# SBUF buffers of a two-layer decoder trunk placed in a stated order, at chosen residues modulo 256 bytes

## The chip, the cores and the metric

The kernel runs on one core of one Trainium2 chip. The time is the device time of one execution in microseconds (us); the kernel before has 1070.82 us as the median of three runs (1070.0 to 1071.1).

## What is computed

The reference is a decoder trunk of two layers over 256 tokens of width 1024, in float32. Each layer merges three token mixers (a convolution module, a top-k sparse attention and a short gated convolution) and adds a gated feed-forward block:

```python
def hybrid_layer(x, ...):
    h = rms_norm(x, norm1_g)
    proj = h @ w_in                      # q, k, v, iq, ik, iw, a, c, g
    ...
    y_attn = dsa_attention(q, k, v, iq, ik, iw) @ w_attn_out
    y_conf = jax.nn.silu(layer_norm(a, conf_ln_g, conf_ln_b)) @ w_conf_out
    y_sc = (c_b * causal_dwconv(c_c * c_x, sc_conv_w)) @ w_sc_out
    merged = gates[:, :, 0] * y_conf + gates[:, :, 1] * y_attn + gates[:, :, 2] * y_sc
    x = x + merged @ w_o
    u = causal_dwconv(rms_norm(x, norm2_g) @ w_up, ffn_conv_w) + ffn_conv_b
    u_gate, u_val = jnp.split(u, 2, axis=-1)
    return x + (jax.nn.silu(u_gate) * u_val) @ w_down
```

All weights together are about 187 MB, and each is read once.

## The kernel before

**Tiles and stages.** Activations stand with features on the 128 partitions and the 256 tokens along the free axis. Every large product is a sum of 128x128 weight tiles times a 128x256 activation tile. The weights come from HBM as a stream of chunks of 128 x 2048 float32 (1 MB each), and each chunk is handled as two halves of eight tiles. ScalarE rounds a half to float32r (`cast`, L406, tile `wh`), VectorE takes the rest (`low`, L363, tile `wl` = raw - wh), and TensorE forms high x high, low x high and high x low, so that three matmuls stand for one float32 product (`fm`). In nearly all stages the weight tile is the stationary operand, which a LDWEIGHTS loads, and the activation tile is the moving one, 256 columns. In the stages IQ, KX, V and Q the two change places.

**Names.** The letters of the matmuls' outputs are the stages: A, IQ, KX, V, Q, C, CB, S, G, T, F, O, U, N, in this order in each layer. The moving tiles are `xgh/xgl` (input of a norm, high and low), `hh/hl` (normed), `sh/sl`, `ah/al`, `cfh/cfl`, `mh/ml` and `uh/ul`.

**Order of the work.** `Plan.add` records every instruction with its inputs, outputs, a cost and a due time, and `Plan.schedule` makes one list schedule of them for PE, ACT, DVE and the DMA queue of SP. A buffer (`Buf`) has a tag, and the schedule gives it a slot of this tag when its first instruction is issued: `raw` has 3 slots, `wh` 6, `wl` 6 (always used in the same turn, `wh_i` with `wl_i`), `big` 8 (activations of 8 KB per partition), `att` 2. `Plan.emit` then asks the tile pool for each buffer under the name of its slot, and writes out the instruction.

**Where a slot stands.** The pool lays its slots one behind another in SBUF, in the order in which a name is first asked for, each start at a multiple of 32 bytes. Before the change this is the order in which the schedule first uses a slot, so that small buffers stand between the large ones. Every address that a matmul reads is a slot's start plus a multiple of 256 bytes (a weight tile is 512 bytes per partition, an activation tile 1024), so that the start of the slot modulo 256 is the residue of all tiles in it. The stage KX is the exception: its tiles are 328 columns (1312 bytes) wide.

Of the kernel before, what the change touches and what calls it, by code (L numbers as in the profile page):

```python
# [9 lines left out]
F32 = mybir.dt.float32  # L10
# [6 lines left out]
P = 128  # L17
# [48 lines left out]
         "m8": 2, "tv": 3, "ty": 3, "tt": 3, "r2": 2, "two": 7, "one": 9, "mx": 2, "sm": 2, "ri": 2}  # L66
SHARED = {"m1": ("one", 5), "rr": ("one", 3), "b1": ("one", 2), "m2": ("two", 3), "rel": ("two", 2), "b2": ("two", 2), "ct": ("two", 2)}
BANKS = ("pm", "pq", "pa")
LOADS = {AF.Sigmoid: "sigmoid", AF.Exp: "exp", AF.Silu: "silu"}
LAT = {("dve", "dve"): 127, ("dve", "act"): 130, ("act", "act"): 143, ("act", "dve"): 143,  # L70
       ("dve", "pe"): 365, ("act", "pe"): 390, ("pe", "dve"): 198, ("pe", "act"): 198, ("pe", "pe"): 0,
# [7 lines left out]


class Buf:
    """A tile of the plan: placed in a slot of its tag when its first instruction is issued."""

    def __init__(self, shape, dtype, tag, name):
        self.shape, self.dtype, self.tag, self.name = list(shape), dtype, tag, name
        n = int(np.prod(shape[1:]))
        grain = n if tag in BANKS else (1 if n <= 64 else 64)
        self.idx = np.arange(n).reshape(shape[1:]) // grain
# [9 lines left out]


class View:  # L100
    """An access pattern of a Buf, built when the instruction is emitted."""

    def __init__(self, buf, chain, idx, shape=None, whole=False):
        self.buf, self.chain, self.idx, self.whole = buf, chain, idx, whole
# [35 lines left out]


class Plan:
    """Records instructions in program order, orders them by a list schedule, and emits them."""

    def __init__(self):
        self.ops = []
# [7 lines left out]
    def add(self, eng, fn, outs, ins, cost, func=None, due=None):  # L154
# [16 lines left out]
        for v in ins:  # L171
            if isinstance(v, View):
                b = v.buf
                op.bufs.append(b)
                bank = b.tag in BANKS
                for c in v.cells():
# [30 lines left out]
    def schedule(self):  # L207
# [51 lines left out]
        while len(done) < len(ops):  # L259
# [25 lines left out]
            cost = o.cost  # L285
            if o.func in LOADS and LOADS[o.func] != table:
                table = LOADS[o.func]
                cost += 1283
# [18 lines left out]
        return done  # L307

    def emit(self, tc, pools):
        for o in self.schedule():  # L310
            for b in o.allocs:
                b.tile = pools[b.tag in BANKS].tile(b.shape, b.dtype, tag=b.slot, name=b.name)
            o.fn()
# [3 lines left out]
def trunk(ctx: ExitStack, tc: tile.TileContext, xt: bass.AP, wst: bass.AP, prm: bass.AP,  # L317
# [39 lines left out]
    def psum(v):  # L357
        return isinstance(v, View) and v.buf.tag in BANKS

# [825 lines left out]
```

## Time and profile before

| | |
|---|---|
| median of 3 runs | 1070.82 us (1070.0 to 1071.1) |
| profiled execution, span from first to last instruction | 1068.2 us |
| PE busy | 1061.8 us, 99% of the span, 8784 matmuls |
| DVE busy | 914.3 us, 86% |
| ACT busy | 702.9 us, 66% |
| DMA | 191.63 MB, 179 GB/s on the mean |
| chain of waits that ended last | PE 98% |

The span is the time between the first and the last instruction of one profiled execution; the device time of a run also holds what lies around it. The page gives no device time of the profiled execution itself; the median of the runs is 2.6 us over its span. Matmuls are pipelined: the duration in a row of PE (some 280 ns) is a latency, and several overlap, so that the rate is read from the starts of successive rows of the timeline.

### The profile page before, as it was taken

To read this page: it belongs to the slowest core of one execution; us is meant where nothing else is said; L and a number is where in the kernel's file an instruction comes from. 1 tells how busy PE (TensorE), PEld (TensorE's weight loads), DVE (VectorE), ACT (ScalarE), POOL (GpSimd) and SP (SyncE) were. 2 spreads that over 40 slices of the span, in tenths; PEclk is the share of its full clock that TensorE was granted. 3 is DMA by queue.
4 is the path that set the end of the run, shared out by engine and by line. 5 is a ranking of instruction groups with operands and counts; after the bars stand their busy time and mean duration, and the time that the engine had idled before them with its cause. 6 is when DMAs were issued, how large, how long until landed. Compare 5 with 4: busy or idle time off the path is not lost.

```text
span 1068.2 us, 21702 instructions
## 1 busy us (share of the span) xinstructions
PE 1061.8 (99%) x8784; PEld 1046.6 (98%) x8784; DVE 914.3 (86%) x1813; ACT 702.9 (66%) x1242; POOL 0.2 (0%) x4
## 2 busy tenths in 40 slices
PE   8999999999999999999999999999999999999998
PEld 8999999999999999999999999999999999999998
DVE  7999999999887899885689999999987789988742
ACT  6868657896565666664466795588857456766531
POOL 0000000000000000000000000000000000000000
PEclk9999999999999999999999999999999999999999
DMA  8665554435655356555455554533464653655550
GB/s 286 222 208 176 170 165 156 153 119 182 214 198 198 119 198 219 182 199 201 171 175 184 205 182 146 201 133 119 163 233 156 204 193 120 222 212 184 179 211 21
DMA packets 29461, 191.63 MB, mean 179 GB/s; under 512 B 3504, under 2 KB 4784, under 8 KB 7088
## 3 DMA queue, kind: packets, MB, share of 16 engines
q1 hardware_dynamic: 29360, 190.23, 51.4%
q8 instruction: 69, 1.13, 0.4%
q14 instruction: 32, 0.26, 0.1%
HBM read 189.17 MB, written 1.05 MB: 178 GB/s over the span
## 4 chain that ended last, share of the span: by engine, by line
PE 98%; DVE 1%; DMA 1%; SPq 0%; issue 0%; ACT 0%; DVEq 0%
PE U L346 23%; PE G L346 13%; PE N L346 12%; PE C L346 9%; PE A L346 8%; PE T L346 4%; PE F L346 4%; PE O L346 4%; PE S L346 4%; PE Q L346 4%; PE CB L346 4%; PE IQ L346 2%; PE KX L346 1%; PE V L346 1%; PE qk L346 1%; PE po L346 1%
## 5 line engine op out<-in xcount | busy, mean ns | idle before, releaser
L363 DVE TENSOR_TENSOR wl<-raw,wh 128x1024 fp32r<-128x1024 f32 (+2 forms) x364 | 432.6, 1198 | 70.1 <-ACT wh L406 68.4
L406 ACT CAST wh<-raw 128x1024 fp32r<-128x1024 f32 (+2 forms) x364 | 369.1, 1030 | 165.6 <-PE N L346 39.5
L346 PE MATMUL U<-hhb,wh 128*128 128x256 f32 x576 | 139.1, 281 | 0.0
L346 PE MATMUL U<-hhb,wl 128*128 128x256 f32 x576 | 139.0, 280 | 0.0
L370 DVE SCALAR_TENSOR_TENSOR acc<-a,psb,acc 128x245 f32<-128x245 f32 (+18 forms) x320 | 132.3, 463 | 0.1
L346 PEld LDWEIGHTS U<-hhb,wl 128*128 128x128 f32 x576 | 108.7, 189 | 0.0
L346 PEld LDWEIGHTS U<-hhb,wh 128*128 128x128 f32 x576 | 108.5, 188 | 0.0
L346 PE MATMUL G<-hha,wh 128*128 128x256 f32 x384 | 94.0, 284 | 0.0
L346 PE MATMUL G<-hha,wl 128*128 128x256 f32 x384 | 92.8, 281 | 0.0
L346 PE MATMUL N<-uh,wh 128*128 128x256 f32 x352 | 83.0, 279 | 0.0
L346 PE MATMUL N<-uh,wl 128*128 128x256 f32 x352 | 83.0, 279 | 0.0
L346 PE MATMUL U<-hlb,wh 128*128 128x256 f32 x576 | 79.1, 280 | 0.0
L370 DVE SCALAR_TENSOR_TENSOR u<-U,psb,u 128x255 f32<-128x255 f32 (+1 forms) x144 | 59.6, 474 | 18.1 <-ACT u L401 18.1
L346 PEld LDWEIGHTS G<-hha,wl 128*128 128x128 f32 x384 | 72.7, 189 | 0.3 <-issue 0.2
L346 PEld LDWEIGHTS G<-hha,wh 128*128 128x128 f32 x384 | 72.5, 189 | 0.3 <-issue 0.2
L346 PEld LDWEIGHTS U<-hlb,wh 128*128 128x128 f32 x576 | 72.7, 188 | 0.0
L401 ACT ACTIVATE ct<-a,psb 128x253 f32<-128x253 f32 (+9 forms) x160 | 70.1, 489 | 0.0
L346 PEld LDWEIGHTS N<-uh,wl 128*128 128x128 f32 x352 | 66.5, 189 | 0.0
L346 PEld LDWEIGHTS N<-uh,wh 128*128 128x128 f32 x352 | 66.5, 189 | 0.0
L346 PE MATMUL C<-hha,wh 128*128 128x256 f32 x256 | 62.8, 285 | 0.0
L346 PE MATMUL C<-hha,wl 128*128 128x256 f32 x256 | 61.8, 280 | 0.0
L401 ACT ACTIVATE u<-U,psb 128x256 f32<-128x256 f32 x72 | 37.2, 560 | 34.3 <-PE U L346 34.3
(259 smaller groups left out, 2600.3 us busy)
## 6 DMA issues: line engine op xcount, KB each, us to landing
raw<-in_w SPq DMA_DIRECT2D x174, 1024.0 KB, 4.8
raw<-in_w SPq DMA_DIRECT2D x4, 656.0 KB, 3.9
raw<-in_w SPq DMA_DIRECT2D x8, 256.0 KB, 6.0
out<-xres SPq DMA_DIRECT2D x8, 128.0 KB, 2.1
xres<-in_xt SPq DMA_DIRECT2D x3, 256.0 KB, 6.3
psb<-in_p SPq DMA_DIRECT2D x2, 277.0 KB, 7.0
csb<-in_c SPq DMA_DIRECT2D x1, 304.0 KB, 8.5
xres<-in_xt SPq DMA_DIRECT2D x2, 128.0 KB, 3.6
```

Of the source, the lines that this page charges most:

```text
L346: nc.tensor.matmul(ap_of(o), ap_of(l), ap_of(r), start=st, stop=sp, skip_group_check=bool(kw))
L363: G.add("dve", lambda: nc.vector.tensor_tensor(ap_of(o), ap_of(a), ap_of(b), op=op), [o], [a, b], (c + n) / 0.96)
L370: G.add("dve", lambda: nc.vector.scalar_tensor_tensor(ap_of(o), ap_of(a), ap_of(s), ap_of(b), op0=op0, op1=op1), [o], [a, s, b], (c + n) / ...
L401: nc.scalar.activation(ap_of(o), ap_of(i), f, **{k: ap_of(v) for k, v in kw.items()})
L406: G.add("act", lambda: nc.scalar.copy(ap_of(o), ap_of(i)), [o], [i], width(o) / 1.2 + 94)
```

## The change

No computation is added, removed or reordered. `emit` first runs the schedule to its end, notes the largest size of each slot, and then asks the pool once for every slot in the order of the new table `LAYOUT`, with fillers between (`gap32` is 32 float32, 128 bytes); slots that the table doesn't name follow in the order of first use. After that the loop over the instructions runs as before and finds every slot at its place. The built programs of before and after have the same instructions in the same order on all five engines, row for row, with the same number of waits; the addresses alone differ.

```diff
@@ -66,6 +66,10 @@
 BANKS = ("pm", "pq", "pa")
+LAYOUT = (["gap32"] + [f"big_{i}" for i in range(4)],
+          ["gap32_b"] + [f"big_{i}" for i in range(4, 8)] + [f"att_{i}" for i in range(2)] + ["kT_0", "vt_0"],
+          ["gap32_c", "wh_0", "wl_0", "gap8_1", "wh_1", "wl_1", "gap8_2", "wh_2", "wl_2", "gap8_3", "wh_3", "wl_3"],
+          ["gap8_4", "wh_4", "wl_4", "gap16_5", "wh_5", "wl_5"])
@@ -307,7 +311,20 @@
     def emit(self, tc, pools):
-        for o in self.schedule():
+        order = self.schedule()
+        size = {}
+        for o in order:
+            for b in o.allocs:
+                if b.tag not in BANKS:
+                    n = int(np.prod(b.shape[1:]))
+                    size[b.slot] = max(size.get(b.slot, 0), n)
+        first = [t for group in LAYOUT for t in group]
+        for slot in first + [t for t in size if t not in first]:
+            if slot.startswith("gap"):
+                pools[0].tile([P, int(slot[3:].split("_")[0])], F32, tag=slot, name=slot)
+            elif slot in size:
+                pools[0].tile([P, size[slot]], F32, tag=slot, name=f"home_{slot}")
+        for o in order:
             for b in o.allocs:
                 b.tile = pools[b.tag in BANKS].tile(b.shape, b.dtype, tag=b.slot, name=b.name)
             o.fn()
```

The residues of the slots' starts modulo 256 bytes, from the two built programs (the eight big slots are named by the first tile that each holds in layer 0):

| slot | before | after |
|---|---|---|
| wh_0, wl_0 | 224, 224 | 0, 0 |
| wh_1, wl_1 | 224, 224 | 32, 32 |
| wh_2, wl_2 | 224, 224 | 64, 64 |
| wh_3, wl_3 | 224, 224 | 96, 96 |
| wh_4, wl_4 | 32, 160 | 128, 128 |
| wh_5, wl_5 | 224, 160 | 192, 192 |
| raw_0, raw_1, raw_2 | 192, 224, 224 | 0, 32, 32 |
| big_0, big_1 (xgh, xgl) | 224 | 0 |
| big_2, big_3 (hh, hl) | 160 | 0 |
| big_4, big_5, big_6 (a, acc, iq) | 160 | 128 |
| big_7 (qt) | 32 | 128 |
| att_0, att_1 (ah, al) | 32 | 128 |

TensorE reads two tiles at a time: the moving tile of the running matmul and the weights of the next one. Call **offset** the residue of the stationary tile that loads next minus the residue of the moving tile, modulo 256. Over the 8,205 neighbouring pairs of float32r matmuls with 256 columns the programs have

| offset | 0 | 32 | 64 | 96 | 128 | 160 | 192 | 224 |
|---|---|---|---|---|---|---|---|---|
| pairs before | 2600 | 0 | 3246 | 0 | 674 | 0 | 1685 | 0 |
| pairs after | 1361 | 787 | 1342 | 827 | 1356 | 595 | 1378 | 559 |

## Rows read from the trace of the kernel before

**Rows 1.** The page: span, busy time, granted clock in 40 slices, chain.
```profile
span 1068.2 us, 21702 instructions
...
PE 1061.8 (99%) x8784; PEld 1046.6 (98%) x8784; DVE 914.3 (86%) x1813; ACT 702.9 (66%) x1242; POOL 0.2 (0%) x4
...
PEclk9999999999999999999999999999999999999999
...
PE 98%; DVE 1%; DMA 1%; SPq 0%; issue 0%; ACT 0%; DVEq 0%
```
**Rows 2.** Waits of PE: who for whom, us in total, times, longest.
```profile
PE pw L346 <- DVE avg L506: 1.0, 1, 1.0
PE A L346 <- ACT xgha L401: 1.0, 1, 1.0
PE A L346 <- DVE wl L363: 0.9, 1, 0.9
```
**Rows 3.** Chain of waits: longest pieces; start us, us, what.
```profile
22.82 34.20 PE A L346 x288
236.44 36.84 PE G L346 x312
359.77 116.59 PE U L346 x992
476.36 61.58 PE N L346 x528
546.31 37.64 PE A L346 x320
886.89 116.71 PE U L346 x992
1003.60 61.43 PE N L346 x528
```
**Rows 4.** PE timeline, stage A, offset 0: start us, us, instruction.
```profile
27.27 0.28 PE L346 MATMUL A<-xgha,wl 128*128 128x256 f32 x1
...
39.86 0.28 PE L346 MATMUL A<-hha,wh 128*128 128x256 f32 x1
```
**Rows 5.** PE timeline, stage G, offset 64.
```profile
246.56 0.28 PE L346 MATMUL G<-hha,wl 128*128 128x256 f32 x1
...
258.93 0.28 PE L346 MATMUL G<-hha,wh 128*128 128x256 f32 x1
```
**Rows 6.** PE timeline, stage N, offset 64.
```profile
509.30 0.28 PE L346 MATMUL N<-uh,wh 128*128 128x256 f32 x1
...
512.02 1.18 PE L346 MATMUL N<-ul,wh 128*128 128x256 f32 x9
```
**Rows 7.** PE timeline, stage G, offset 128.
```profile
260.85 1.11 PE L346 MATMUL G<-hla,wh 128*128 128x256 f32 x8
261.80 0.28 PE L346 MATMUL G<-hha,wh 128*128 128x256 f32 x1
```
**Rows 8.** PE timeline, stage T of layer 1, offset 192.
```profile
810.55 0.28 PE L346 MATMUL T<-ah,wh 128*128 128x256 f32 x1
...
821.86 0.28 PE L346 MATMUL T<-ah,wh 128*128 128x256 f32 x1
```
**Rows 9.** PE timeline, stage KX (328 columns), every sixth matmul.
```profile
71.50 0.32 PE L346 MATMUL KX<-wh,hha 128*128 128x328 f32 x1
...
72.39 0.31 PE L346 MATMUL KX<-wh,hha 128*128 128x328 f32 x1
...
73.29 0.31 PE L346 MATMUL KX<-wh,hha 128*128 128x328 f32 x1
...
74.18 0.32 PE L346 MATMUL KX<-wh,hha 128*128 128x328 f32 x1
...
75.10 0.28 PE L346 MATMUL V<-wh,hha 128*128 128x256 f32 x1
```
**Rows 10.** PE timeline: first and last row of the float32r matmuls.
```profile
6.71 0.58 PE L346 MATMUL A<-xgha,wh 128*128 128x256 f32 x1 [1.04 <-ACT xgha L401]
...
1063.79 1.23 PE L346 MATMUL N<-ul,wh 128*128 128x256 f32 x9
```
**Rows 11.** Instructions that write wl and wh: duration ns min/median/max.
```profile
L363 DVE TENSOR_TENSOR wl<-raw,wh x364: 680/1217/1228, 6.0 to 1050.7; 128x1024 fp32r<-128x1024 f32 x174, 128x512 fp32r<-128x512 f32 x4, 128x656 fp32r<-128x656 f32 x4
L406 ACT CAST wh<-raw x364: 603/1047/1077, 5.3 to 1049.3; 128x1024 fp32r<-128x1024 f32 x174, 128x512 fp32r<-128x512 f32 x4, 128x656 fp32r<-128x656 f32 x4
```

## The prediction

> **What bounds the kernel now.** Read the page first [rows 1]: PE is busy 99% of the span, the chain that ended last is PE for 98%, and the granted clock is 9 in all forty slices, its upper level of 2.4 GHz. The waits of PE confirm it [rows 2]: three, 2.9 us together, all at the start. So no load, cast or subtraction holds TensorE up; the kernel is as long as 8,784 matmuls take one after the other. The chain shows at what pace [rows 3]: its seven longest pieces hold 3,960 matmuls in 464.99 us, 117.4 ns each, but they differ: 118.8 ns in the first piece of A, 118.1 in G, 117.5 in U, 116.6 and 116.3 in N. All are the same instruction, 128x128 weights and 256 columns. What differs is where their operands stand.
>
> The timeline of PE shows it, stretch by stretch. Take starts that follow each other and divide by the matmuls between them (counted in the program). Offset 0, stage A: 105 matmuls from 27.27 to 39.86, 119.9 ns each [rows 4]. Offset 192, stage T: 96 in 11.31 us, 117.8 ns [rows 8]. Offset 128: eight in 0.95 us, 118.8 ns [rows 7]. Offset 64 has two paces: 105 in 12.37 us, 117.8 ns, in G [rows 5], and 24 in 2.72 us, 113.3 ns, in N [rows 6]. Both kinds last for dozens of matmuls; which one a stretch falls into, the offset alone does not say.
>
> Over all starts between the first and the last row [rows 10], sorted by offset and without gaps over 140 ns (8,136 intervals), the means are 118.67 ns at offset 0 (2,562 of them), 116.23 at 64 (3,230), 118.93 at 128 (674) and 117.42 at 192 (1,670). I use these four; the stretches above show their spread.
>
> **The change part by part.** *Fillers and home tiles.* They issue no instruction: zero on every engine and queue.
>
> *Residues of raw, wh and wl for ScalarE and VectorE.* Before, `raw` stands at 192 and 224 and `wh` at 224 and 32, so VectorE already reads four combinations; yet its subtractions run 1217 ns in the median and 1228 at most, the casts 1047 and 1077 [rows 11]. They don't see residues. I cost this at nothing. The cover is PE: VectorE is busy 86% of the time, so that even 3% on each subtraction would still leave PE the bound.
>
> *Residues for TensorE.* This is the whole change, and its price is pairs times nanoseconds. Before: 2600 x 118.67 + 3246 x 116.23 + 674 x 118.93 + 1685 x 117.42 = 963.84 us. After, the four known offsets: 1361 x 118.67 + 1342 x 116.23 + 1356 x 118.93 + 1378 x 117.42 = 640.57 us for 5,437 pairs. Within them the trade is poor: 1,239 pairs leave the dear offset 0, but 1,904 leave 64, the cheapest, and 682 are added at 128, the dearest. The other 2,768 pairs go to 32, 96, 160 and 224, which no stage of this width has now. Their pace u decides: the break-even is (963.84 - 640.57) / 2768 = 116.8 ns.
>
> Bounds for u, from the nearest rows: below, 113.3 ns, the best pace held anywhere for a stretch [rows 6]; above, 119.9 ns, the worst [rows 4]. The first gives 640.57 + 313.61 - 963.84 = -9.7 us, the second 640.57 + 331.88 - 963.84 = +8.6 us. Between them I take the mean of the four known offsets, 117.8 ns, since each new one lies midway between two of them. That is +326.1 us, and the sum +2.8 us.
>
> One stage lets the new offsets be seen, at another width: in KX every second tile of 328 columns starts 32 bytes further round. In groups of six matmuls [rows 9] the first group (offsets 128 and 0) has 148 ns each, the second (96 and 224) 150, the third (192 and 0) 148, the fourth (160 and 224) 153. The new offsets are no cheaper there, rather 2 to 5 ns dearer. At 328 columns the load of the weights is hidden for longer, so I take the direction as a hint and not the size. It speaks against u near 113.
>
> Weigh this against a rule. The rows say that two tiles read at once cost each other up to 6.6 ns per matmul, by where they stand [rows 4, 6]. The Trainium skill says otherwise: "Loading the next tile's weights doesn't steal SBUF read bandwidth from the running matmul" (page "TensorE: Matmul & The Clock Gate", section "Step-by-step: what each phase is for"), because PE has two independent read ports. By that sentence the sum would be zero; by the rows it is +2.8 us. I go by the rows, since the same stationary and moving shapes at the same granted clock differ by 6%, and leave the rule as a rival.
>
> The sum is made on the profiled execution: 1068.2 + 2.8 = 1071.0 us of span. The median of the runs is 2.6 us over that span, so the forecast is 1073.6 us. A measurement of this kernel can tell about 0.2% (2.1 us) from no change, so the forecast stands just outside it.
>
> **The rivals.**
>
> *A, the new offsets are the good ones (faster).* The place is the 2,768 pairs at odd multiples of 32; the price is 2,768 x (116.8 - u), so that it decides from u = 116.0 downward, where the gain passes 2.1 us. At the fast pace of 113.3 the time is 1070.8 - 9.7 = 1061.1 us; if offset 64 also ran always at its fast pace, 1342 x (116.23 - 113.3) = 3.9 us more go, 1057.2. For it: the pace of 113.3 exists and holds for whole stretches, offset 64 and 192 both are cheaper than 0 and 128, so distance seems to help, and nothing shows that 64 is the best. Against it: KX, and that the new offsets are no farther apart than 64.
>
> *B, the new offsets are as dear as 0, and offset 64 loses its fast pace (slower by more).* 8.6 us from u = 119.9, and 1342 x (117.8 - 116.23) = 2.1 us from offset 64, together +10.7: 1081.5 us. For it: the fast stretch of N comes right behind one at offset 0 and lasts while the offset stays [rows 6]; six residues in turn change the offset every 24 matmuls. Against: it needs all new offsets to be at the worst value seen.
>
> *C, the pace does not hang on residues.* The differences would then be the stages' own, by order and neighbours, and the time stays at 1070.8 us. For it: offset 64 has two paces [rows 5, 6] with nothing moved. Against: offsets 0, 128 and 192 keep theirs in different stages of both layers. The skill's rule on the read ports, above, is this case.
>
> That the change doesn't do what it says I leave out: the built program has the stated residues.
>
> **How the numbers follow.** The forecast's own case is u between 116.0 and 118.8, -2.1 to +5.6 us, 1068.7 to 1076.4: 0.48, of which 0.20 within 0.2% and 0.28 slower. A has 0.34 (faster), B 0.12 (slower), C 0.06 (same). Hence faster 0.34, same 0.26, slower 0.40. The range reaches from A at its fast pace nearly to B: 1060 to 1080 leaves out the case that offset 64 gets fast as well, and the upper end of B.
>
> **What would show it.** Right: PE still 99% busy with no new wait; the paces of offsets 0, 128 and 192 within 1 ns of those above; stretches at 32, 96, 160 and 224 between 116 and 119 ns; subtractions still 1217 ns. The stages that had offset 64 most, G, C and O of layer 0, with weights now at six residues, lose a little of what the first A gains. Wrong: a stretch of a new offset at 113 ns or under (A), paces that are alike for all offsets (C), or a PE that waits for VectorE.

## The result and the profile after

The changed kernel takes 1077.43 us (median of 4 runs, 1076.92 to 1077.63), the kernel before 1070.59 in the same job (4 runs, 1070.0 to 1071.1). The ratio is 1.0061 with a 95% interval of 1.0046 to 1.0075: slower by 0.6%, +6.8 us. The forecast was slower by 2.8 us. The direction held, and the time lies within the range, just over the forecast's own case (up to 1076.4); the size forecast was less than half of what came.

The page of the changed kernel (span, busy time, granted clock, chain) reads as before [rows 1]:

```profile
span 1075.7 us, 21702 instructions
...
PE 1068.0 (99%) x8784; PEld 1052.8 (98%) x8784; DVE 915.1 (85%) x1813; ACT 703.0 (65%) x1242; POOL 0.2 (0%) x4
...
PEclk9999999999999999999999999999999999999999
...
PE 98%; DMA 1%; DVE 0%; SPq 0%; ACT 0%; issue 0%
```

The waits of PE (who for whom, us in total, times, longest), beside [rows 2]:

```profile
PE A L363 <- ACT xgha L418: 3.2, 2, 2.6
PE pw L363 <- DVE avg L523: 1.0, 1, 1.0
PE A L363 <- DVE wl L380: 0.3, 1, 0.3
```

And the instructions that write `wl` and `wh` (ns, min/median/max), beside [rows 11]:

```profile
L380 DVE TENSOR_TENSOR wl<-raw,wh x364: 682/1220/1239, 5.5 to 1058.0; 128x1024 fp32r<-128x1024 f32 x174, 128x512 fp32r<-128x512 f32 x4, 128x656 fp32r<-128x656 f32 x4
L423 ACT CAST wh<-raw x364: 605/1046/1072, 4.9 to 1056.5; 128x1024 fp32r<-128x1024 f32 x174, 128x512 fp32r<-128x512 f32 x4, 128x656 fp32r<-128x656 f32 x4
```

PE is still the bound, at the upper clock, and waits only at the start. VectorE and ScalarE take as long as they did (1220 against 1217 ns, 1046 against 1047). So the time went into the matmuls' pace. The longest pieces of the chain (start us, us, what), beside [rows 3], show where:

```profile
23.73 34.06 PE A L363 x288
238.48 36.76 PE G L363 x312
362.16 117.56 PE U L363 x992
479.72 62.31 PE N L363 x528
550.51 37.82 PE A L363 x320
892.65 117.51 PE U L363 x992
1010.16 62.38 PE N L363 x528
```

The first A and G are 0.1 us shorter, the second A 0.2 longer; U loses 1.0 and 0.8 us, N 0.7 and 0.95. Together the seven take 3.4 us more, 118.3 ns a matmul instead of 117.4; the rest is spread over the shorter pieces.

Over the whole program, sorted as in the prediction (starts that follow each other, gaps over 140 ns left out; 8,133 intervals), the mean goes from 117.47 to 118.25 ns. Over 8,205 pairs that is +6.4 of the +7.5 us by which the spans of the two profiled executions differ. Most of the other 1.1 us lies at the start: PE waits 4.5 us there against 2.9, and the first long piece of A starts at 23.73 us against 22.82. This wait changes from execution to execution without following the pace: for the first `xgha` PE waited 3.7 us in the run e1 below, which has the pace of before, and 1.2 us in e12, which is slower than the change. So I put it to the start and not to the residues, which is likely but not shown.

| offset | 0 | 32 | 64 | 96 | 128 | 160 | 192 | 224 |
|---|---|---|---|---|---|---|---|---|
| before, ns | 118.67 | | 116.23 | | 118.93 | | 117.42 | |
| after, ns | 119.50 | 118.23 | 116.44 | 118.67 | 118.68 | 119.66 | 117.77 | 117.53 |

One stage shows most of it in a row. In stage O of layer 1 the moving tile stands at 0 and the weights run through the slots 0, 1, 2, 3, 4, 5, so that 24 matmuls each see one offset. The PE timeline of the changed kernel there (start us, us, instruction; first of each 24, and the first behind the last):

```profile
867.03 0.28 PE L363 MATMUL O<-mh,wh 128*128 128x256 f32 x1
...
869.91 0.28 PE L363 MATMUL O<-mh,wh 128*128 128x256 f32 x1
...
872.75 0.28 PE L363 MATMUL O<-mh,wh 128*128 128x256 f32 x1
...
875.49 0.28 PE L363 MATMUL O<-mh,wh 128*128 128x256 f32 x1
...
878.38 0.28 PE L363 MATMUL O<-mh,wh 128*128 128x256 f32 x1
...
881.22 0.28 PE L363 MATMUL O<-mh,wh 128*128 128x256 f32 x1
...
884.04 0.28 PE L363 MATMUL U<-xghb,wh 128*128 128x256 f32 x1
```

The differences are 2.88, 2.84, 2.74, 2.89, 2.84 and 2.82 us; by 24: 120.0 ns at offset 0, 118.3 at 32, 114.2 at 64, 120.4 at 96, 118.3 at 128, 117.5 at 192. One slot of six is fast, and the one behind it is the slowest. For offset 160 stage T of layer 1 gives 24 matmuls in 2.88 us, 120.0 ns:

```profile
818.79 0.28 PE L363 MATMUL T<-ah,wh 128*128 128x256 f32 x1
...
821.67 0.28 PE L363 MATMUL T<-ah,wh 128*128 128x256 f32 x1
```

### The profile page after: what moved, and what is told of

Its sections match the earlier page's. It is cut to its first block, busy times and chain, and to the rows that moved or that the text cites. A ratio compares the mean times of both kernels' runs of the same rounds, so it can differ in the third digit from the quotient of the medians.

```text
span 1075.7 us, 21702 instructions
## 1 busy us (share of the span) xinstructions
PE 1068.0 (99%) x8784; PEld 1052.8 (98%) x8784; DVE 915.1 (85%) x1813; ACT 703.0 (65%) x1242; POOL 0.2 (0%) x4
## 3 DMA queue, kind: packets, MB, share of 16 engines
HBM read 189.17 MB, written 1.05 MB: 177 GB/s over the span
## 4 chain that ended last, share of the span: by engine, by line
PE 98%; DMA 1%; DVE 0%; SPq 0%; ACT 0%; issue 0%
PE U L363 23%; PE G L363 13%; PE N L363 12%; PE C L363 9%; PE A L363 8%; PE T L363 4%; PE Q L363 4%; PE S L363 4%; PE O L363 4%; PE F L363 4%; PE CB L363 4%; PE IQ L363 2%; PE KX L363 1%; PE V L363 1%; PE qk L363 1%; PE po L363 1%
```

## The experiments

The theory: the offset alone sets the pace of a matmul, so that the time of a placement is pairs times the pace of their offsets. The rival: it is the place, the order in SBUF, the home tiles or the stages' own mix, and the offsets only go along with it. All kernels are the changed kernel with another table `LAYOUT`; instructions and their order are the same in all. Of most edits only the new lines are shown. ACTS stands below for `[f"big_{i}" for i in range(8)] + ["att_0", "att_1", "kT_0", "vt_0"]`, all at one residue (128 in the built programs); with it the offset in nearly all stages is how far the weights' residue lies beyond that. Where the weights move (V, Q) it is the negative of this. The last column has means by offset, sorted as above, of the offsets with over 800 intervals. Each kernel ran four times, e1, e10 and e11 ten times.

| run | median us (range) | ratio to before, 95% | ns by offset |
|---|---|---|---|
| e1 | 1070.57 (1069.4 to 1072.24) | 0.9996 [0.9987, 1.0005] | 0: 118.68, 64: 116.08, 128: 118.90, 192: 117.53 |
| e2 | 1060.82 (1059.82 to 1062.42) | 0.9907 [0.9892, 0.9921] | 64: 116.19 |
| e3 | 1042.73 (1042.33 to 1044.63) | 0.974 [0.9725, 0.9754] | 64: 113.76, 192: 114.28 |
| e4 | 1090.86 (1090.81 to 1091.12) | 1.0186 [1.0169, 1.0203] | 0: 119.96 |
| e5 | 1076.47 (1076.08 to 1077.25) | 1.0053 [1.0038, 1.0068] | 0: 119.65, 32: 118.21, 64: 116.30, 96: 118.40, 128: 118.47, 192: 117.78 |
| e6 | 1088.43 (1087.95 to 1089.9) | 1.0167 [1.015, 1.0184] | 0: 119.75, 128: 118.89 |
| e7 | 1076.33 (1075.71 to 1077.28) | 1.0052 [1.0037, 1.0067] | 32: 117.87, 160: 118.64 |
| e8 | 1041.77 (1041.65 to 1044.4) | 0.9734 [0.9719, 0.9748] | 64: 114.01, 192: 113.88 |
| e9 | 1045.06 (1043.84 to 1046.22) | 0.976 [0.9746, 0.9775] | 64: 114.01, 192: 116.27 |
| e10 | 1068.97 (1068.5 to 1069.77) | 0.9985 [0.9976, 0.9995] | 192: 117.44 |
| e11 | 1068.55 (1067.37 to 1069.79) | 0.9979 [0.997, 0.9989] | 224: 117.01 |
| e12 | 1090.14 (1089.94 to 1090.45) | 1.0182 [1.0167, 1.0197] | 160: 119.98 |

The kernel before had 1070.99 us beside e1 to e4 (13 runs), 1070.68 beside e5 to e8 (7), 1070.74 beside e9 to e12 (19).

**e1: the stated order, with the residues of before.**

```diff
+LAYOUT = (["gap40", "big_7", "att_0", "att_1"],
+          ["gap32"] + [f"big_{i}" for i in range(2, 7)] + ["wl_4", "wl_5"],
+          ["gap16_a", "big_0", "big_1"] + [f"{w}_{i}" for i in range(4) for w in ("wh", "wl")] + ["wh_5"],
+          ["gap16_b", "wh_4"])
```

> Slots grouped and asked for in a stated order as in the changed kernel, but each large slot at the residue modulo 256 that it has before the change (offset counts as before: 2600 pairs at 0, 3246 at 64, 674 at 128, 1685 at 192). Theory (the residues alone set the pace): the time of before, 1070.6 us, within 2 us. Rival (the place in SBUF or the order of the slots matters, or the home tiles cost something): the time of the changed kernel, 1077, or another one over 2 us away from before.

No difference, to 0.1%. U and N take what they take before [rows 3] to the hundredth, in layer 0 as here and in layer 1; the long pieces of A and G differ by up to 0.2 us:

```profile
359.75 116.59 PE U L363 x992
476.34 61.58 PE N L363 x528
```

So order, place and home tiles cost nothing: all of the change is its residues.

Two more rivals can be read from the built programs. One is the residue of `raw`, which moves along with the fillers. It does not sort the times: it stands at 0 and 32 in the changed kernel, e2 and e8 (1077.4, 1060.8 and 1041.8 us) and at 128 and 160 in e3, e5, e9 and e10 (1042.7, 1076.5, 1045.1 and 1069.0). The other is the residue of one tile alone in place of the difference of two. In the changed kernel the same offset has nearly the same mean with the moving tile at 0 and at 128: 119.6 and 119.3 ns at offset 0, 118.6 and 118.8 at 128, 117.8 and 117.7 at 192; at 64, with its two paces, 116.2 and 116.9.

**e2: all weights at offset 64.**

```diff
+LAYOUT = (ACTS, ["gap16"] + [f"{w}_{i}" for i in range(6) for w in ("wh", "wl")])
```

> All activation slots at one residue and all twelve weight slots 64 bytes further, so that 7731 of 8205 pairs have offset 64. Theory (pace by offset, class means of the two traces, 116.2 to 116.4 ns at 64): about 11 us under before, 1059 to 1061; at the fast pace of 113.3 ns throughout 1039, at the slow one of 117.8 ns throughout 1073. Rival (the pace comes from the mixture or from the stage, not from the offset): within 3 us of 1070.6.

10 us faster than before. But offset 64 keeps its two paces. Pieces of its chain (start us, us, what), the stage F in layer 0 and in layer 1, and the long piece of U that follows in each:

```profile
304.02 22.61 PE F L361 x192
...
357.58 116.84 PE U L361 x992
...
826.62 21.76 PE F L361 x192
...
878.42 116.83 PE U L361 x992
```

F has the same residues in both layers (its activations are in other slots) and 117.8 ns a matmul in the one, 113.3 in the other; both of these pieces of U run at 117.8. In layer 1, 144 pairs of addresses (moving tile and next weights) come in F and again in U: the same two places ran at 113.3 ns in F and at 117.8 in U. So at this offset something besides the addresses decides, and the theory, by which the offset alone sets the pace, does not hold at 64. The PE timeline shows where a stretch changes over:

```profile
351.56 0.28 PE L361 MATMUL U<-xghb,wh 128*128 128x256 f32 x1
...
353.09 0.28 PE L361 MATMUL U<-xghb,wl 128*128 128x256 f32 x1
353.21 0.50 PE L361 MATMUL msb<-avg,sqb 128*128 128x1 f32 x4
...
354.48 0.28 PE L361 MATMUL U<-xghb,wh 128*128 128x256 f32 x1
...
356.40 0.28 PE L361 MATMUL U<-xghb,wl 128*128 128x256 f32 x1
...
356.97 0.60 PE L361 MATMUL prb<-csb,r2b 128*128 128x128 f32 x4
```

13 intervals from 351.56 to 353.09 at 117.7 ns, then the four small matmuls of `msb`; 17 intervals from 354.48 to 356.40 at 112.9; then the four of `prb`, and the 992 of U above at 117.8. An interruption can put the stream from one pace to the other, and it stays there: in none of the 52 stretches without a gap (nine intervals or more) does a run of eight fast intervals (under 115.5 ns) begin or end more than four matmuls behind the start of the stretch.

**e3: high weights at 64, low weights at 192.**

```diff
+LAYOUT = (ACTS, ["gap16_h"] + [f"wh_{i}" for i in range(6)], ["gap32_l"] + [f"wl_{i}" for i in range(6)])
```

> As the kernel with all weights at offset 64, but the low halves at 192: high 64, low 192, 5300 pairs at 64 and 2901 at 192, which alternate while high and low weights take turns. By the class means alone 8 us under before, 1063. In the trace of before the one weight pair that stood so against the activations of stage A and U (offsets 64 and 192 in turn) ran mostly at 113.3 to 114 ns; if alternating is what holds the fast pace, the turn stretches run at 113.5 and the time falls to 1045 to 1055, under the kernel with all at 64. Rival (offset plays no part): 1070.6 within 3 us.

28 us faster than before, beyond what was expected. Its page (span, busy time) and chain:

```profile
span 1041.0 us, 21702 instructions
...
PE 1032.6 (99%) x8784; PEld 1017.6 (98%) x8784; DVE 912.4 (88%) x1813; ACT 700.8 (67%) x1242; POOL 0.2 (0%) x4
```

```profile
75.08 2.83 PE V L362 x24
...
90.75 11.31 PE Q L362 x96
...
352.76 112.48 PE U L362 x992
465.24 59.84 PE N L362 x528
```

U and N run at 113.4 and 113.3 ns; 91% of the intervals at offset 64 and 83% of those at 192 are under 115.5, 88% of all, where before 40% and 17% were, 23% of all. V and Q, where the weights move, have 64 and 192 in turn too, and stay at 117.8 to 117.9 ns: none of their intervals is fast.

**e4: all weights at offset 0.**

```diff
+LAYOUT = (ACTS, [f"{w}_{i}" for i in range(6) for w in ("wh", "wl")])
```

> All activation and all weight slots at one residue, every pair at offset 0: the suspected cost at its fullest. Theory: 118.7 to 119.9 ns for each of 8205 pairs, 10 to 20 us over before, 1081 to 1091. Rival (the pace comes from having several residues): under or at 1070.6.

20 us slower than before, 120 ns throughout; only 8 of 8,147 intervals are under 115.5 ns. Its chain:

```profile
366.17 119.03 PE U L361 x992
485.21 63.36 PE N L361 x528
```

Between e3 and e4 lie 48 us: the same 21,702 instructions, a granted clock of 0.998 and 1.000, other addresses.

**e5 and e6: the parts of the change by themselves.** e5 has the weights of the change and the activations at one residue; e6 has the activations of the change and all weights at 0.

```diff
# e5
-LAYOUT = (["gap32"] + [f"big_{i}" for i in range(4)],
-          ["gap32_b"] + [f"big_{i}" for i in range(4, 8)] + [f"att_{i}" for i in range(2)] + ["kT_0", "vt_0"],
-          ["gap32_c", "wh_0", "wl_0", "gap8_1", ...],
+LAYOUT = (ACTS, ["wh_0", "wl_0", "gap8_1", ...],
           ["gap8_4", "wh_4", "wl_4", "gap16_5", "wh_5", "wl_5"])
# e6
-          ["gap32_c", "wh_0", "wl_0", "gap8_1", ...],
-          ["gap8_4", "wh_4", "wl_4", "gap16_5", "wh_5", "wl_5"])
+          ["gap32_c"] + [f"{w}_{i}" for i in range(6) for w in ("wh", "wl")])
```

> One part of the change alone: the six weight pairs at 0, 32, 64, 96, 128 and 192, all activation slots at one residue (offsets 0, 32, 64, 96, 128 and 192 with some 1300 pairs each). Theory (pairs times the class means of the changed kernel): 3 us over before, 1072 to 1078, so that this part is the change's cost. Rival (the two residues of the activations make it dear): within 2 us of 1070.6.

> The other part alone: activations at the two residues of the change, all weights at one (5386 pairs at offset 0, 2819 at 128). Theory: 119.96 and 118.7 ns, 12 to 17 us over before, 1083 to 1087, a little under the kernel with all at offset 0 (1090.9). Rival (a second residue as such helps): under 1075.

The six residues of the weights alone cost 5.8 us of the 6.8: the activations' second residue adds little to them. With all weights at one residue the two residues of the activations cost 17.8 us, 2.1 less than the 19.9 of e4 with one residue for all (e6 came out 1.4 us above what was expected). So the parts don't add up; what each does hangs on the offsets that it makes with the other.

**e7 and e8: is it any two offsets 128 apart?** e7 has high weights at 32 and low at 160, e8 turns e3 about: high at 192, low at 64.

```diff
# e7
+LAYOUT = (ACTS, ["gap8_h"] + [f"wh_{i}" for i in range(6)], ["gap32_l"] + [f"wl_{i}" for i in range(6)])
# e8
+LAYOUT = (ACTS, ["gap48_h"] + [f"wh_{i}" for i in range(6)], ["gap32_l"] + [f"wl_{i}" for i in range(6)])
```

> High weights at offset 32, low at 160: they stand 128 bytes apart as in the kernel at 64 and 192, but both moved 32 bytes back. Theory 1 (two weight residues 128 bytes apart hold the fast pace): near that kernel, 1042 to 1050. Theory 2 (the offsets 64 and 192 themselves are needed; class means 118.2 and 119.7): 1075 to 1080.

> The kernel at 64 and 192 with high and low exchanged, so that the matmuls with the low activations (a third, high weights only) stand at 192 in place of 64. Theory (the alternation holds the fast pace and stretches that follow keep it): 1042 to 1050. Rival (the third with high weights only takes the pace of its own offset, 117.8 ns at 192): 2570 matmuls at 117.8 in place of 113.7, 10 us over the other, 1053.

e7 is as slow as the change, e8 as fast as e3:

```profile
354.26 112.50 PE U L362 x992
466.75 59.84 PE N L362 x528
```

Two offsets 128 apart are not enough: of 32 with 160 no eight intervals in a row are under 115.5 ns. Nor are they in any run at 0, 32, 96, 128, 160 or 224, but for a few intervals at the edge of a fast stretch at 64 or 192. In e8 the matmuls of the low activations, which read `wh` alone and so have 192 without turning, run at 113.6 ns. V and Q, where the weights move, stay slow here too (117.8 ns).

**e9: does one turning half keep the others fast?** As e2, but `wl_5` at 192 (and the low slots behind the high ones, as in e3): one pair of slots in six alternates, the others stay at 64.

```diff
+LAYOUT = (ACTS, ["gap16_h"] + [f"wh_{i}" for i in range(6)] + [f"wl_{i}" for i in range(5)], ["gap32_l", "wl_5"])
```

> All weights at offset 64 but the low half of the sixth pair, which stands at 192: only one half in six alternates between 64 and 192. Theory 1 (the alternation brings TensorE into a fast state, and a stretch at constant offset 64 keeps the state it is entered in): the five halves that follow run at 113.3 to 114 ns too, 1042 to 1050. Theory 2 (only the matmuls of an alternating stretch are fast): a sixth of the way from the kernel all at 64 (1060.8) to the alternating one (1042.7), 1057 to 1058.

26 us faster than before, 16 than e2, from the residue of one tile moved by 128 bytes. Its chain:

```profile
353.37 112.69 PE U L362 x992
466.06 59.84 PE N L362 x528
```

U goes from 117.8 to 113.6 ns, with five of its six slot pairs at 64 as in e2. The timeline at the start of this piece shows the change:

```profile
354.16 0.28 PE L362 MATMUL U<-xghb,wh 128*128 128x256 f32 x1
...
359.81 0.28 PE L362 MATMUL U<-xghb,wh 128*128 128x256 f32 x1
359.93 0.28 PE L362 MATMUL U<-xghb,wl 128*128 128x256 f32 x1
...
362.54 0.28 PE L362 MATMUL U<-xghb,wh 128*128 128x256 f32 x1
...
367.98 0.28 PE L362 MATMUL U<-xghb,wh 128*128 128x256 f32 x1
```

The 48 matmuls up to 359.81 take 117.7 ns each. The row at 359.93 is the first of the piece that has `wl_5`. The 48 from 362.54, at offset 64 again, take 113.3. In the whole run 14 stretches go from slow to fast more than four matmuls behind their start, and all 14 do so within four matmuls of a load of `wl_5`; in e2 none does. So the turn from 64 to 192 brings the fast pace where the activations move, and a stretch at 64 keeps it. In V and Q of e3 and e8 the turn did not bring it; why is open.

**e10, e11, e12: one offset for all weights, 192, 224 and 160.** The filler ahead of the weights in e2 becomes 48, 56 and 40 float32.

> All activations at one residue, all weights at offset 192 (7731 pairs). Theory (class means 117.4 to 117.8, no alternation that would bring the fast state): 1068 to 1073. If a constant 192 finds the fast state by itself as often as a constant 64 does: near 1061.

> All weights at offset 224, the cheapest of the four new offsets by the class means of the changed kernel (117.5). Theory: 1066 to 1073. If the class mean there came from the neighbours in the sequence: up to 1088, the pace of offset 0.

> All weights at offset 160, the dearest of the four new offsets by the class means of the changed kernel (119.7). Theory: 15 to 20 us over before, 1085 to 1091. If the class mean came from the neighbours in the sequence: 1070 to 1078.

192 alone gives no gain to speak of (117.44 ns, 8% of the intervals fast), 224 the same, and 160 is as dear as 0: U takes 119.04 us in e12, 119.03 in e4. The first long pieces of V in e10, e11 and e12, and of U in e12, in this order:

```profile
76.16 2.75 PE V L361 x24
```

```profile
75.18 2.84 PE V L361 x24
```

```profile
75.79 2.85 PE V L361 x24
...
365.32 119.04 PE U L361 x992
```

No kernel has 32 or 96 throughout, but V and Q have the negative offset: 64 in e10, 32 in e11, 96 in e12. Over the 462 intervals of each the means are 113.7, 118.4 and 118.4 ns. So 64 alone also ran fast there, in 94% of the intervals, with nothing taking turns.

## Why the prediction was right in direction and short in size

*What costs nothing: right.* Fillers, home tiles and order cost nothing (e1). The casts and subtractions don't see residues: their medians are 1217 to 1220 and 1046 to 1047 ns in all fourteen kernels.

*That the offset of the two tiles TensorE reads sets the price: right in the main, but not alone.* e1 holds it with order and places changed; e4 and e12 against e3 give it 48 us. At 64 and 192 it leaves two paces open (e2, e9). Rival C, and the rule of the Trainium skill on two read ports (page "TensorE: Matmul & The Clock Gate", section "Step-by-step: what each phase is for"), would have all twelve kernels at 1070.8 us; they lie between 1041.8 and 1090.9.

*The term u, the new offsets: mis-sized.* It was taken as 117.8 ns, the mean of the known ones, "since each new one lies midway between two of them". Measured: 118.23, 118.67, 119.66 and 117.53 ns at 32, 96, 160 and 224. With their pairs this is 787 x 0.43 + 827 x 0.87 + 595 x 1.86 - 559 x 0.27 = 2,013 ns: 2.0 us more. All four lie above the break-even of 116.8 ns, so the direction does not hang on one of them. The pace is no smooth function of the offset: 160 lies between 128 and 192, whose means are 118.7 and 117.8, and is as dear as 0 (e12). The rows that spoke to it were there, in KX, though [rows 9] alone show less than the prediction read from them: to the nanosecond the four groups take 149.3, 149.7, 148.3 and 152.7 ns, so that only the group with 160 stands out, by 3 to 4 ns. The groups ahead of them in the same trace, at 192 and 160 in turn, take 150.3, 151.2, 151.0 and 152.3.

*The terms of the four known offsets: taken as constants, which they are not.* 0 came out 0.83 ns dearer, 64 0.21, 192 0.35, 128 0.25 cheaper: 1361 x 0.83 + 1342 x 0.21 + 1378 x 0.35 - 1356 x 0.25 = 1,555 ns, 1.6 us. At 64 and 192 a class mean before was a mixture of two lasting paces, and the share of fast intervals fell: at 64 from 40% to 32, at 192 from 17 to 5. The clearest case is N of layer 0: before, 298 of 527 intervals were at 64, with a mean of 115.2 ns; after, 98 of 527 are, with 117.5. Offset 0, the largest part (1.1 us), has no fast stretch in either trace; its mean is 118.67 before, 119.50 after and 119.96 alone in e4. That what stands beside it makes the difference is likely, but not shown. With stretches at 64 cut down to one slot in six, less was fast: stretches of eight fast intervals or more hold 12% of the intervals before and 5% after. That was the second half of rival B, in part; its first half is true of 160 alone. Together 2.8 + 2.0 + 1.6 = 6.4 us, the pace's whole share. The way from 1073.6 to 1077.43 us is then 2.0 + 1.6 + 1.1 for the start, less 0.9: the prediction put the median 2.6 us over the profiled span, and after the change it lies 1.7 us over it.

*The stages named: right, but not where most was lost.* Over all their intervals C, G and O of layer 0 lost 0.34, 0.16 and 0.04 us, together twice the 0.26 that the first A gained. The long piece of G lost nothing (36.76 against 36.84 us): its stretch at 64 was at the slow pace already [rows 5]. Over half of the 6.4 us went in U (1.05 and 0.82 us) and N (0.74 and 0.94). N had 42 and 45% of its intervals under 115.5 ns before and 11% after, U 16 and 25% before, 7 and 8% after.

*The paces forecast.* 128 and 192 stayed within 1 ns, 0 too in the mean (0.83); the stretches at 96 and 160, at 120.4 and 120.0, left the band of 116 to 119.

*Rival A: refuted.* It needed u under 116.0. Alone, 160 has 119.98 ns and 224 has 117.01, and in the change 32 and 96 have 118.2 and 118.7. What its argument drew on, that 113.3 exists and can be held, was true, but of 64 and 192, not of the new offsets.

The start's 1.1 us was not in the forecast; it is seen in the two profiled executions alone, as the other runs left no trace.

What beats both kernels is in the same table: e8 at 1041.77 us, 0.9734 [0.9719, 0.9748] of before, and e3 beside it.

## What to carry to other kernels

When PE is 99% busy and waits for nothing, still divide the starts in its timeline by the number of matmuls: the same instruction at the same clock ran at 113.3 to 120.0 ns here, by where its two SBUF operands stand modulo 256 bytes and, at offsets 64 and 192, by what ran before. Spreading buffers over many residues was no remedy here; choose the offset between stationary and moving tile, measure each candidate by a kernel that has it alone, and try pairs that alternate, since the best placement (64 with 192) can't be read from either alone. And a class mean from a trace is only a price if the class has one pace: look at its spread before multiplying.

## What was not expected of the hardware

- At offset 64 the stream of matmuls has two lasting paces, 113.3 and 117.8 ns, with nothing moved (e2: 113.3 in F and 117.8 in U of layer 1 at 144 shared pairs of addresses). Four small matmuls in between can change the one for the other.
- Alternating between 64 and 192 brings the fast pace where the activations move (e3, 88% of all intervals), and one weight slot in six that does so is enough for most of it (e9, 1045.06 us against 1060.82). Where the weights move (V and Q of e3 and e8) it does not.
- Offsets 0 and 160 cost the same 120.0 ns and had no fast stretch in e4 and e12; 224, the mirror image of 32, is cheaper than it (117.0 ns against 118.4, both in e11).

What TensorE or SBUF does to make two paces, and why 64 and 192 of all offsets have the fast one, stays open: the runs show when it comes and that it stays, not why.
